# Hybrid encoder layer: first transfers in a held order, head norm weights spread on chip, first norms, value weights, bridge operands and closing sums reordered

## The chip, the cores and the metric

One core of a Trainium2 chip runs the kernel. It has a matrix engine (PE, TensorE) and three engines for the rest: DVE (VectorE), ACT (ScalarE) and POOL (GpSimd). SP (SyncE) issues most transfers, ACT some. Each engine works through its own instructions in order, and waits on semaphores for the others. The metric is the device time of one execution, in microseconds; lower is better.

## The reference

One layer of a pre-norm encoder, applied to two inputs with the same weights: `x_prompt` (1024 tokens) and `x_sample` (512 tokens), 1024 wide, float32.

```python
def _token_mixer(xn, w_in, q_norm_g, k_norm_g, rpb, w_proj_a, w_proj_b, w_out):
    z = xn @ w_in
    qa, ka, va, qb, kb, vb, ga, gb = jnp.split(z, idx, axis=-1)
    qa = _apply_rope(_rmsnorm(qa, q_norm_g), cos, sin)     # 8 heads of 64
    ka = _apply_rope(_rmsnorm(ka, k_norm_g), cos, sin)     # 2 heads
    o_a = _gqa_attention(qa, ka, va)                       # over all tokens
    o_b = _neighbourhood_attention(qb, kb, vb, rpb)        # 8 x 16 window, learned bias
    merged = jax.nn.sigmoid(ga) * (o_a @ w_proj_a) + jax.nn.sigmoid(gb) * (o_b @ w_proj_b)
    return merged @ w_out

def _trunk(x, ...):
    h = x + _token_mixer(_rmsnorm(x, norm_mix_g), ...)
    h = h + jnp.square(jax.nn.relu(_rmsnorm(h, norm_mlp_g) @ w_mlp_up)) @ w_mlp_down   # 4096 wide
    return _rmsnorm(h, norm_final_g)
```

## The kernel before

**Products.** Every product of float32 operands is three products on PE (`mm3`, lines 158 to 161). Each operand is split into a high half, rounded by a copy on ACT, and a low half, the difference, by a subtraction on DVE (`split`, lines 147 to 156; `cut`, 1074 to 1076, in the MLP). The three are high by high (L159), high by low and low by high (L160, L161).

**Trunks.** `run` handles a trunk: trunk 0 is `x_sample` (four tiles of 128 tokens; `first` is true), trunk 1 `x_prompt` (eight tiles). The profile's names read alike for both, so they are told apart by their times. Four stages follow each other in each:

- First (`phR`), in two groups of heads g = 0, 1: for each tile tt of 128 tokens the norm (`norm_tile`: squares summed on ACT, L214; `ms` on DVE, L142; the power on POOL, L144; the scaled tile `xn` on DVE, L218), eight transposes on PE into `ptx` (L232), and the split of these into `xs_0h` (ACT, L242) and `xs_0l` (DVE, L246). Then the product `z` with the weights of queries and keys, loaded by `load_a` (`rawq`, `rawkv`; halves `wgh`, `wgl`); the head norm (`sq` and `ssA` on ACT, L530; `ms_A`; `t` on DVE, L534, with the table `gtab`); the rotation with the rope tile `rt` (L552 to L554, result `rr`); and `heads_t`, transposes of `rr` into `pq` (L468). The key for the values is cut from `z` as `vhl` (L537, L538); that is the last reader of a tile's `z` and frees its PSUM buffer, of which there are four. `values` multiplies by the value weights that `load_v` loads (`raw_v`; halves `wh_v`, `wl_v`) into `zv`.
- Global attention (`phA`), with products of the gates as filling work for PE (`Fill`).
- Neighbourhood attention (`phB`): `load_qk(pr)` loads and splits the weights of a pair of heads (`raw_bq`, `raw_bk`; `w_bq`, `w_bk`), `qkproj` multiplies, and 32 units, four per head, run `s_unit` (scores `sb`, maximum, exponential `pb`, its sum's reciprocal `rlb` on DVE, L804, and `pb` scaled on POOL, L805), `t_unit` (transposes `ptb`, L817) and `v_unit`. Gate products `gps` with `w_gs` fill PE between.
- Projections, output weights and norms (`phG`).

**MLP.** `mlp` takes both trunks' 1536 tokens as two blocks of 768. `run_up(b, ...)` makes the up product of a block in 16 slices, as a scheme of seven smaller products (`ua` to `ud`) whose operands `A` and `B` are sums of blocks; what comes out (`c`, `cs`) goes to memory as `ud`. Between the blocks stands a **bridge** (lines 1384 to 1413): for q = 0, 1, 2 `pair_t` transposes a piece of the second block's `B` (`pt`, L270), and two of the down scheme's product 5, `dnf`, are made. Their operands come by `a_dma` (`ar`, from `ud`) and `a_step` (halves `ah`, `al`, L1075 and L1076). `last_of(0)` returns the steps that the last slice of the first block runs beside its products. After the second block come the down scheme's products in the order 5, 3, 1, 6, 7, 4, 2, with `gain` adding each result to the stream `h`, and `final`, `final_half` and `final_rest` making the closing norm.

**What sets the order.** The program is written for a tile scheduler, which builds each engine's list from the text's order, dependences and its own priorities; `tc.keep_in_program_order` holds an instruction at its place. A transfer waits at SP until its buffer is free, and until an earlier transfer, eight back, has landed, since each uses one of eight semaphores in turn.

**At the start** SP issues `xts_0` (tile 0), the norm weights, the query weights, `xts_1`, `rawkvs`, the head norm weights into `gtab` (the query's row of 64 read for 128 partitions and four heads), `raw_vs`, the first rope tile and only then `x23s` (tiles 2 and 3).

## Time and profile before

| what | us |
|---|---|
| median of three runs | 2198.17 (2197.47 to 2203.12) |
| the profiled execution | 2196.47 |
| its span, first to last instruction | 2194.7 |
| PE busy | 2137.7 |
| DVE busy | 1456.9 |
| ACT busy | 1111.3 |
| POOL busy | 348.0 |
| mean granted clock of PE | 0.994 |

How to read it: a row of a group or of the timeline names the line, the engine, the operation, `out<-in`, and in brackets the engine's idle time just before, with what ended it. The view of waits lists for PE which operation waited for which, the us in total, how often, and the longest. A row of the windows gives busy time of PE, its weight loads, DVE, ACT and POOL in a stretch, each with its count, then the granted clock of PE, the share of DMA time and GB/s. Times count from the start of the span. Line numbers are those of the kernel before.

### The profile page before, as it was taken

The page shows a single profiled execution, that of the slowest core. Times are in us where ns is not written, and L with a number is a line of the kernel's source. Part 1 is how long each engine was busy: PE and PEld are TensorE (multiplying, and loading weights), DVE is VectorE, ACT ScalarE, POOL GpSimd, SP SyncE. Part 2 cuts the span into 40 slices and gives each one's busy share as a digit, 9 for nine tenths or more (in the row PEclk, how much of TensorE's full clock was granted, in tenths as well). Part 3 has the DMA queues.
Part 4 walks back from the last instruction along what each step waited for, and adds up shares of the span by engine and source line. Part 5 has one row for each costly group of instructions (what it writes and reads, how often), then busy time and mean ns, then how long its engine had stood idle before and what let it go on. Part 6 is the DMA issues. An engine that isn't in the chain of part 4 may idle for free. (4 is left out here: it accounts for less than half of the span.)

```text
span 2194.7 us, 32408 instructions
## 1 busy us (share of the span) xinstructions
PE 2137.7 (97%) x11180; PEld 1869.9 (85%) x11180; DVE 1456.9 (66%) x2835; ACT 1111.3 (51%) x2377; POOL 348.0 (16%) x458
## 2 busy tenths in 40 slices
PE   6999999999999999999999999999999999999998
PEld 6787877898898888888888899997999988888886
DVE  5755567577756755545773777777777777769663
ACT  4645554456635655545531466665655543433452
POOL 2232120333333223223300200003000000000000
PEclk8999999999999999999999999999999999999999
DMA  5525548530122124324363556568544699788551
GB/s 150 165 84 156 150 138 270 196 91 30 44 68 90 42 60 126 97 84 125 122 200 136 199 181 192 175 226 205 172 142 157 214 351 341 235 275 282 178 193 67
DMA packets 320299, 351.56 MB, mean 160 GB/s; under 512 B 31751, under 2 KB 255623, under 8 KB 320135
## 3 DMA queue, kind: packets, MB, share of 16 engines
q1 hardware_dynamic: 278455, 280.27, 41.0%
q10 hardware_dynamic: 36000, 52.18, 6.8%
q0 software_dynamic: 5680, 17.04, 2.8%
q8 instruction: 88, 1.44, 0.3%
q14 instruction: 76, 0.62, 0.1%
HBM read 265.47 MB, written 87.88 MB: 161 GB/s over the span
## 5 line engine op out<-in xcount | busy, mean ns | idle before, releaser
L161 PE MATMUL dn<-wd,al 128*128 128x512 f32 x624 | 242.8, 389 | 0.0
L160 PE MATMUL dn<-wd,ah 128*128 128x512 f32 x624 | 242.8, 389 | 0.0
L159 PE MATMUL dn<-wd,ah 128*128 128x512 f32 x624 | 242.7, 389 | 0.0
L1075 ACT ACTIVATE ah<-ar 128x512 fp32r<-128x512 f32 x168 | 104.1, 628 | 197.6 <-PE dn L160 184.8
L1076 DVE TENSOR_TENSOR al<-ar,ah 128x512 fp32r<-128x512 f32 x168 | 115.4, 695 | 71.1 <-ACT ah L1075 61.7
L161 PEld LDWEIGHTS dn<-wd,al 128*128 128x128 f32 x624 | 117.1, 188 | 24.5
L159 PEld LDWEIGHTS dn<-wd,ah 128*128 128x128 f32 x624 | 117.1, 188 | 24.3
L160 PEld LDWEIGHTS dn<-wd,ah 128*128 128x128 f32 x624 | 117.1, 188 | 24.2
L634 DVE TENSOR_TENSOR ptls<-pTs,pths 128x512 fp32r<-128x512 f32 x160 | 107.5, 686 | 38.2 <-ACT pths L633 37.5
L594 POOL TENSOR_SCALAR ps<-ps,rls 128x1024 f32<-128x1024 f32 (+1 forms) x96 | 96.3, 1005 | 223.6 <-DVE rls L593 213.3
L633 ACT ACTIVATE pths<-pTs 128x512 fp32r<-128x512 f32 x160 | 94.2, 598 | 74.2 <-PE pTs L628 71.8
L588 DVE TENSOR_REDUCE nms<-ss 128x1 f32<-128x1024 f32 (+1 forms) x96 | 99.5, 1040 | 25.3 <-PE ss L586 25.3
L159 PE MATMUL gpss<-xs_0h,w_gs 128*128 128x512 f32 x256 | 106.1, 414 | 2.8 <-ACT sgs L363 1.3
L591 ACT ACTIVATE ps<-ss,nms 128x1024 f32<-128x1024 f32 (+1 forms) x96 | 93.3, 973 | 23.7 <-DVE nms L588 21.3
L628 PEld LDWEIGHTS pTs<-ident,ps 128*128 128x128 f32 x640 | 78.0, 140 | 29.0 <-POOL ps L594 4.5
L161 PE MATMUL gpss<-xs_0h,w_gs 128*128 128x512 f32 x256 | 101.6, 397 | 0.1
L160 PE MATMUL gpss<-xs_0l,w_gs 128*128 128x512 f32 x256 | 101.3, 396 | 0.0
L628 PE MATMUL pTs<-ident,ps 128*128 128x128 f32 x640 | 98.9, 274 | 1.3 <-DVE ptls L634 0.3
L144 POOL TENSOR_TENSOR rs_f<-ms_f,mhalf 128x1 f32<-128x1 f32 x6 | 4.0, 669 | 590.8 <-DVE ms_f L142 590.8
L805 POOL TENSOR_SCALAR pbs<-pbs,rlbs 128x384 f32<-128x384 f32 (+1 forms) x96 | 56.3, 592 | 226.0 <-DVE rlbs L804 211.7
L1076 DVE TENSOR_TENSOR A<-S,A 128x512 fp32r<-128x512 f32 x128 | 84.5, 686 | 9.6 <-ACT A L1075 9.4
L1075 ACT ACTIVATE A<-S 128x512 fp32r<-128x512 f32 x128 | 75.6, 623 | 29.5 <-DVE S L1138 21.6
(299 smaller groups left out, 6432.6 us busy)
## 6 DMA issues: line engine op xcount, KB each, us to landing
ar<-ud SPq DMA_DIRECT2D x120, 512.0 KB
br<-in_w_mlp_down_dram SPq DMA_DIRECT2D x72, 512.0 KB
rawu<-in_w_mlp_up_dram SPq DMA_DIRECT2D x64, 512.0 KB
ud<-c ACTq DMA_DIRECT2D x128, 192.0 KB
raw_gs<-in_w_in_dram SPq DMA_DIRECT2D x32, 512.0 KB
zgs<-sgs ACTq DMA_DIRECT2D x48, 256.0 KB
ud<-cs SPq DMA_DIRECT2D x64, 192.0 KB
raw_os<-in_w_out_dram SPq DMA_DIRECT2D x16, 512.0 KB
```

Of the source, the lines that this page charges most:

```text
L159: nc.tensor.matmul(out, ah, bh, start=start, stop=False, **kw)
L160: nc.tensor.matmul(out, ah, bl, start=False, stop=False, **kw)
L161: nc.tensor.matmul(out, al, bh, start=False, stop=stop, **kw)
L588: nc.vector.tensor_reduce(nm_, s, axis=AX.X, op=ALU.max, negate=True)
L591: nc.scalar.activation(p, s, AF.Exp, bias=nm_, accum_out=l)
L594: nc.gpsimd.tensor_scalar(p, p, rl, 1.0, op0=ALU.mult, op1=ALU.mult)
L628: nc.tensor.transpose(pt[:, j * P : (j + 1) * P], PP[u, j][:, kc * P : (kc + 1) * P], ident)
L633: nc.scalar.activation(hi, pt, AF.Copy)
L634: nc.vector.tensor_tensor(lo, pt, hi.bitcast(F32), op=ALU.subtract)
L805: nc.gpsimd.tensor_scalar(p, p, rl, 1.0, op0=ALU.mult, op1=ALU.mult)
L1075: nc.scalar.activation(hi, src, AF.Copy)
L1076: nc.vector.tensor_tensor(lo, src, hi.bitcast(F32), op=ALU.subtract)
```

## The change

It has five parts.

- **Start, trunk 0.** `x23s` is held in place and issued behind `rawkvs`; the norm of tile 1 is written ahead of the split of `rawkvs`. The query's head norm weights are loaded once as `gq` (64 per partition), and the multiplication that fills `gtab` reads them broadcast over four heads. Several first transfers are held in program order.
- **Value weights, trunk 1.** Their splits are collected in `hold` and run after tile 0's rotation; the norm of tile 4, the first that is made there, comes after tile 1's rotation.
- **Neighbourhood attention.** `load_qk(1)` moves from ahead of unit 0 to unit 3.
- **Bridge.** The last slice of the first block makes four operands of product 5 instead of two; each step of the bridge issues the next step's loads ahead of `pair_t` and splits its operands a step ahead.
- **Closing sums.** `final_rest` is cut in two, and its scaling runs after the next `gain`.

```diff
     def setup_tables():
-        row_bcast(gtab[:, 0:4, :], w["a_q_norm_g"], HD, 4)
-        row_bcast(gtab[:, 4:5, :], w["a_k_norm_g"], HD, 1)
+        gq = sgp.tile([P, 512], F32, tag="sg", name="gq", bufs=2)[:, 0:HD].rearrange("p (o d) -> p o d", o=1)
+        tc.keep_in_program_order(row_bcast(gq, w["a_q_norm_g"], HD))
+        tc.keep_in_program_order(row_bcast(gtab[:, 4:5, :], w["a_k_norm_g"], HD))
         tc.keep_in_program_order(
-            nc.vector.tensor_scalar(gtab[:, 0:4, :], gtab[:, 0:4, :], 0.125, None, op0=ALU.mult)
+            nc.vector.tensor_scalar(gtab[:, 0:4, :], gq.to_broadcast([P, 4, HD]), 0.125, None, op0=ALU.mult)
         )
...
-            split(hi[:, kk : kk + kn, :], lo[:, kk : kk + kn, :], rv)
+            cut = partial(split, hi[:, kk : kk + kn, :], lo[:, kk : kk + kn, :], rv)
+            if hold is None:
+                cut()
+            else:
+                hold.append(cut)
...
-                    xn_of[tr.ready] = norm_tile(xt, gb, ph, f"{N}_{tr.ready}")
+                    if first:
+                        xn_of[0] = norm_tile(xt, gb, ph, f"{N}_0")
...
+                    def more_and_norm():
+                        more_x()
+                        xn_of[1] = tr.p0(1, ph, gb, x1.pop())
+
-                    wh, wl = load_a(g, lambda: x1.append(norm_load(x, 1, ph, f"{N}_1")), first_tile, more_x)
+                    wh, wl = load_a(g, lambda: x1.append(norm_load(x, 1, ph, f"{N}_1")), first_tile, more_and_norm)
...
-                if first and fresh:
-                    xn_of[1] = tr.p0(1, ph, gb, x1.pop())
...
                     rr_of[tt] = rr
+                    while held:
+                        held.pop(0)()
+                    if fresh and not first and tt == 1:
+                        xn_of[tr.ready] = norm_tile(xt, gb, ph, f"{N}_{tr.ready}")
...
-            wqk = load_qk(1)
...
+                if i == 3:
+                    wqk = load_qk(1)
...
-                        more = [lambda: a_step(5, 0, 0), lambda: a_step(5, 0, 1)]
+                        more = [lambda g_=g_, j=j: a_step(5, g_, j) for g_ in range(2) for j in range(2)]
...
         for q in range(3):
+            if q < 2:
+                for g in range(2):
+                    a_dma(5, g, q + 1)
             pair_t(f"1_{q}", q, hn.pop(q), B, [bank(f"pt1_{q}_{i}") for i in range(4)], t2)
...
-                    n = 4 * q + 2 * g + i + 2
-                    if n < 12:
-                        a_step(5, n // 2 % 2, n // 4 * 2 + n % 2)
+                    if q < 2:
+                        a_step(5, g, j + 2)
...
-                    final_rest(NTB + j)
+                    final_rest(NTB + j, scales)
+        while scales:
+            scales.pop(0)()
```

What the scheduler makes of it is seen in the engines' lists. First SP at the start of the program, before (the names are those of the text above; `in_...` are inputs):

```order
L207 DMA xts_1_159<-in_x_sample_dram 128x1024
L404 DMA rawkvs_0_197<-in_w_in_dram 128x8x64 x2
L108 DMA gtab<-in_a_q_norm_g_dram 128x4x64
L108 DMA gtab<-in_a_k_norm_g_dram 128x64
L183 DMA raw_vs_0_0_220<-in_w_in_dram 128x4x256
L183 DMA raw_vs_0_4_227<-in_w_in_dram 128x4x256
L506 DMA rts_0_0_257<-in_rope_dram 128x128
L444 DMA x23s_200<-in_x_sample_dram 128x1024 x2
L506 DMA rts_0_1_355<-in_rope_dram 128x128
```

And now:

```order
L216 DMA xts_1_159<-in_x_sample_dram 128x1024
L413 DMA rawkvs_0_197<-in_w_in_dram 128x8x64 x2
L455 DMA x23s_200<-in_x_sample_dram 128x1024 x2
L109 DMA gq<-in_a_q_norm_g_dram 128x64
L109 DMA gtab<-in_a_k_norm_g_dram 128x64
L186 DMA raw_vs_0_0_221<-in_w_in_dram 128x4x256
L186 DMA raw_vs_0_4_228<-in_w_in_dram 128x4x256
L522 DMA rts_0_0_258<-in_rope_dram 128x128
L522 DMA rts_0_1_356<-in_rope_dram 128x128
```

`x23s` has moved ahead of both head norm weights, the value weights and the first rope tile, and the query's row is 128x64 instead of 128x4x64. ACT at the same place, before (`L148` and `L150` are the split's copy, `L214` and `L223` a norm's squares, `L242` and `L251` the split of a transposed tile, `L530` and `L548` the sums of the head norm):

```order
L148 ACTIVATE wghs_0_0_151<-rawkvs_0_197 128x4x128
L148 ACTIVATE wghs_0_1_155<-rawkvs_0_197 128x4x128
L214 ACTIVATE xns_1_209,sss_1_210<-xts_1_159 128x1024
L148 ACTIVATE wh_vs_0_0_222<-raw_vs_0_0_220 128x1024
L148 ACTIVATE wh_vs_0_0_222<-raw_vs_0_4_227 128x1024
L214 ACTIVATE xns_2_249,sss_2_250<-x23s_200 128x1024
L242 ACTIVATE xs_0h_167<-ptxs_1_236 128x4x128
L242 ACTIVATE xs_0h_168<-ptxs_1_236 128x4x128
L530 ACTIVATE sqs_0_0_308,ssAs_0_0_309<-zs_0_0_259 128x64 x5
L242 ACTIVATE xs_0h_167<-ptxs_2_334 128x4x128
```

And now:

```order
L223 ACTIVATE xns_1_203,sss_1_204<-xts_1_159 128x1024
L150 ACTIVATE wghs_0_0_151<-rawkvs_0_197 128x4x128
L150 ACTIVATE wghs_0_1_155<-rawkvs_0_197 128x4x128
L251 ACTIVATE xs_0h_167<-ptxs_1_237 128x4x128
L251 ACTIVATE xs_0h_168<-ptxs_1_237 128x4x128
L223 ACTIVATE xns_2_250,sss_2_251<-x23s_200 128x1024
L150 ACTIVATE wh_vs_0_0_223<-raw_vs_0_0_221 128x1024
L150 ACTIVATE wh_vs_0_0_223<-raw_vs_0_4_228 128x1024
L548 ACTIVATE sqs_0_0_309,ssAs_0_0_310<-zs_0_0_260 128x64 x5
L251 ACTIVATE xs_0h_167<-ptxs_2_335 128x4x128
```

Tile 1's norm stands ahead of the splits of `rawkvs`, its split ahead of tile 2's norm, and the value weights (`wh_vs`) behind both. On DVE the multiplication of `gtab` and tile 2's `xn` likewise stand behind tile 1's split and ahead of the value weights' low halves. The second place is DVE at the start of trunk 1, before:

```order
L154 TENSOR_TENSOR wl_vs_0_0_4791<-raw_vs_0_0_4788,wh_vs_0_0_4790 128x512 x2
L154 TENSOR_TENSOR wl_vs_0_0_4791<-raw_vs_0_4_4795,wh_vs_0_0_4790 128x512 x2
L142 TENSOR_SCALAR ms_s_4_4760<-sss_4_4758 128x1
L218 SCALAR_TENSOR_TENSOR xns_4_4757<-xts_4_4754,rs_s_4_4762,gbs_4753 128x1024
L142 TENSOR_SCALAR ms_As_0_0_4838<-ssAs_0_0_4832 128x5
L534 SCALAR_TENSOR_TENSOR ts_0_0_4842<-zs_0_0_4806,rs_As_0_0_4840,gtab 128x64 x5
L142 TENSOR_SCALAR ms_As_0_1_4891<-ssAs_0_1_4885 128x5
L495 TENSOR_TENSOR vts_0_0_4962<-zvs_0_0_4937,vts_0_0_4962 128x4x64
L538 TENSOR_TENSOR vhls_0_4803<-zs_0_0_4806,vhls_0_4803 128x64
L552 TENSOR_TENSOR ts_0_0_4842<-ts_0_0_4842,rts_0_0_4804 128x320
```

And now:

```order
L144 TENSOR_SCALAR ms_As_0_0_4825<-ssAs_0_0_4819 128x5
L552 SCALAR_TENSOR_TENSOR ts_0_0_4829<-zs_0_0_4793,rs_As_0_0_4827,gtab 128x64 x5
L156 TENSOR_TENSOR wl_vs_0_0_4784<-raw_vs_0_0_4781,wh_vs_0_0_4783 128x512
L556 TENSOR_TENSOR vhls_0_4790<-zs_0_0_4793,vhls_0_4790 128x64
L156 TENSOR_TENSOR wl_vs_0_0_4784<-raw_vs_0_0_4781,wh_vs_0_0_4783 128x512
L156 TENSOR_TENSOR wl_vs_0_0_4784<-raw_vs_0_4_4785,wh_vs_0_0_4783 128x512
L570 TENSOR_TENSOR ts_0_0_4829<-ts_0_0_4829,rts_0_0_4791 128x320
L156 TENSOR_TENSOR wl_vs_0_0_4784<-raw_vs_0_4_4785,wh_vs_0_0_4783 128x512
L572 TENSOR_TENSOR rrs_0_0_4841<-ts_0_0_4829,us_0_0_4837 128x320
```

The low halves `wl_vs` have moved from ahead of tile 0's head norm to places between it and its rotation, tile 4's norm (`xns_4`) to behind these rows; on ACT tile 0's sums likewise now stand ahead of the copies `wh_vs`. The third place is DVE in the neighbourhood attention of trunk 0, before:

```order
L797 ISA sbss_0_1_0_2286,nmbs_0_1_0_2287<-sbs_0_1_2281,bms_0_1_0_2282 128x256
L797 ISA nmbs_0_1_0_2287 128x1
L762 TENSOR_TENSOR kBs_0_1_2200<-pkbs_0_0_2236,kBs_0_1_2200 64x512 x2
L154 TENSOR_TENSOR w_bqs_1_2271<-raw_bqs_1_0_2269,w_bqs_1_2271 128x512 x2
L154 TENSOR_TENSOR w_bks_1_2277<-raw_bks_1_0_2275,w_bks_1_2277 128x512 x2
L804 RECIPROCAL rlbs_0_1_0_2292<-lbs_0_1_0_2290 128x1
L154 TENSOR_TENSOR w_gs_3328_1_2316<-raw_gs_3328_1_0_2314,w_gs_3328_1_2316 128x512 x2
```

And now:

```order
L819 ISA sbss_0_1_0_2275,nmbs_0_1_0_2276<-sbs_0_1_2270,bms_0_1_0_2271 128x256
L819 ISA nmbs_0_1_0_2276 128x1
L784 TENSOR_TENSOR kBs_0_1_2201<-pkbs_0_0_2237,kBs_0_1_2201 64x512 x2
L826 RECIPROCAL rlbs_0_1_0_2281<-lbs_0_1_0_2279 128x1
L819 ISA sbss_0_2_0_2328,nmbs_0_2_0_2329<-sbs_0_2_2325,bms_0_1_0_2271 128x256
L819 ISA nmbs_0_2_0_2329 128x1
L156 TENSOR_TENSOR w_gs_3328_1_2305<-raw_gs_3328_1_0_2303,w_gs_3328_1_2305 128x512 x2
L826 RECIPROCAL rlbs_0_2_0_2334<-lbs_0_2_0_2332 128x1
```

The splits of the next pair's weights no longer stand ahead of the first reciprocal; those of two gates' weights and of `w_bqs_1` follow behind it. In the bridge the low halves `al` of the second and the later steps now stand ahead of the products that use them by a whole step. On DVE, ACT, POOL and SP the list of the closing sums (`gain`, the sums, the scaling) is the same before and after.

## The prediction, made before the changed kernel was run

> **What bounds the kernel now.** The page's first part says whose time it is:

> ```profile
> PE 2137.7 (97%) x11180; PEld 1869.9 (85%) x11180; DVE 1456.9 (66%) x2835; ACT 1111.3 (51%) x2377; POOL 348.0 (16%) x458
> ```

> PE is busy for 97% of the span, so an edit pays only where PE stands idle or runs slowly. The number of matrix products does not change. I therefore went to the waits of PE (columns: total us, times, longest us):

> ```profile
> PE ptxs L232 <- DVE xns L218: 13.8, 4, 10.5
> PE zs L159 <- DVE vts L495: 3.9, 1, 3.9
> PE dnf L161 <- DVE al L1076: 2.9, 3, 1.5
> PE ptbs L817 <- POOL pbs L805: 2.4, 2, 1.4
> ...
> PE gpss L159 <- ACT w_gs L148: 0.7, 1, 0.7
> ```

> The first four rows are the sites of the diff: first norms, value weights, bridge, neighbourhood attention; the last belongs to the fourth. Then I read the timeline around each, and the windows for the granted clock (PEclk, third column from the right). A drop of it is a second price of a gap.

> **Start: first norms and transfers.** The queue of SP, then ACT, DVE and PE (start, duration; in brackets the idle time before and its releaser):

> ```profile
> 3.43 3.76 SPq L404 DMA_DIRECT2D rawkvs<-in_w_in_dram  x2
> 7.23 3.54 SPq L108 DMA_DIRECT2D gtab<-in_a_q_norm_g_dram  x1
> ...
> 17.04 1.49 SPq L444 DMA_DIRECT2D x23s<-in_x_sample_dram  x2
> ```
> ```profile
> 10.65 1.07 ACT L242 ACTIVATE xs_0h<-ptxs 128x512 fp32r<-128x512 f32 x2
> 13.12 1.15 ACT L148 ACTIVATE wghs<-rawkvs 128x512 fp32r<-128x512 f32 x2 [1.41 <-DMA rawkvs<-in_w_in_dram]
> 14.18 1.05 ACT L214 ACTIVATE xns<-xts 128x1024 f32<-128x1024 f32 x1
> ...
> 22.03 1.06 ACT L148 ACTIVATE wh_vs<-raw_vs 128x1024 fp32r<-128x1024 f32 x1 [6.71 <-DMA raw_vs<-in_w_in_dram]
> ...
> 25.85 1.06 ACT L214 ACTIVATE xns<-x23s 128x1024 f32<-128x1024 f32 x1 [1.29 <-DMA x23s<-in_x_sample_dram]
> ```
> ```profile
> 20.43 0.29 DVE L114 TENSOR_SCALAR gtab<-gtab 128x256 f32<-128x256 f32 x1 [2.98 <-DMA gtab<-in_a_q_norm_g_dram]
> ...
> 28.01 1.29 DVE L246 TENSOR_TENSOR xs_0l<-ptxs,xs_0h 128x512 fp32r<-128x512 f32 x2 [2.12 <-ACT xs_0h L242]
> ...
> 30.02 1.28 DVE L218 SCALAR_TENSOR_TENSOR xns<-x23s,rs_s,gbs 128x1024 f32<-128x1024 f32 x1 [0.66 <-POOL rs_s L144]
> ```
> ```profile
> 31.36 1.97 PE L232 MATMUL ptxs<-ident,xns 128*128 128x128 f32 x8 [10.51 <-DVE xns L218]
> ```
> ```profile
> 20.85:31.36 10.51, 0.01 (x2) 0.01 (x1) 5.28 (x9) 5.26 (x16) 0.55 (x1) 0.56 0.88 260
> 31.36:36.00 4.64, 4.64 (x18) 4.64 (x19) 2.13 (x9) 2.24 (x5) 2.34 (x3) 0.54 0.00 0
> ```

> PE has multiplied tile 0 and stands for 10.51 us until tile 2's norm is there, because `x23s` was issued only at 17.04. The next 4.64 us ran at 0.54 of the clock: 4.64 x 0.46 = 2.1 us more. After the change `x23s` follows `rawkvs`, at about 7.2. Its 1.05 MB at the window's 260 GB/s take 4.0 us; behind weights used at 13.12 they are there at 15 to 17. What is late next is ACT and DVE, in the new order:
> - Tile 1's Square follows `xs_0h` at 11.7 instead of 14.18, so its norm (1.05, then sum and power, 0.8 from 29.21 to 30.02 for tile 2, then 1.28) ends near 15. Its own split now stands ahead of tile 2's norm: transposes about 1.0, `xs_0h` 1.07, to 17.5; then Square 1.06 with `xs_0l` beside it, 0.8, and `xns` 1.28 behind the 0.29 of L114. Tile 2 is ready at about 21.2, and PE starts it 31.36 - 21.2 = **10.2** earlier, with a wait of 1 to 2 us in place of 10.51.
> - A wait of that size cost no clock at the bridge and some at the neighbourhood attention (both below): I take the **2.1** back whole, and 0 as the lower end.
> - `wh_vs` (two times 1.06) stand on ACT ahead of the heads' sums and of tile 2's split. If `raw_vs` lands near 22 as now, tile 2's low half is about **1.5** late for PE, and tile 3's norm, queued behind the same work, about **1**.

> 10.2 + 2.1 - 1.5 - 1 = **9.8 us**. Bounds: 12.3 without the last two; 4 if tile 2 lands 4 us later (the whole 1 MB once more) and no clock comes back. Broadcasting on DVE costs nothing I can price: L114 keeps its 128x256 output at 0.29 us, and `xns` is the only work behind it that PE awaits.

> **Value weights, trunk 1.** ACT, DVE, PE, and the window behind:

> ```profile
> 422.44 2.01 ACT L148 ACTIVATE wh_vs<-raw_vs 128x1024 fp32r<-128x1024 f32 x2
> 425.52 1.06 ACT L214 ACTIVATE xns<-xts 128x1024 f32<-128x1024 f32 x1 [1.07 <-DMA xts<-in_x_prompt_dram]
> ```
> ```profile
> 423.79 2.49 DVE L154 TENSOR_TENSOR wl_vs<-raw_vs,wh_vs 128x512 fp32r<-128x512 f32 x4
> ...
> 431.68 0.21 DVE L538 TENSOR_TENSOR vhls<-zs,vhls 128x64 fp32r<-128x64 f32 x1
> ```
> ```profile
> 431.81 0.69 PE L159 MATMUL zs<-wghs,xs_0h 128*128 128x384 f32 x1 [3.85 <-DVE vts L495]
> ```
> ```profile
> 431.81:436.00 4.19, 4.19 (x20) 3.78 (x20) 2.16 (x10) 1.44 (x4) 2.91 (x5) 0.62 0.42 137
> ```

> Tile 3's product needs the accumulator of tile 0, freed by `vhls` at 431.68, because tile 0's head sums wait on ACT behind `wh_vs` and tile 4's Square, which waited for its DMA. At stake: 3.85 + 4.19 x 0.38 = 5.4 us. Now the sums come first, 4 us earlier, and free it near 427.5. But the low halves of the value weights now stand on DVE behind tile 0's scaling and, the last, behind its rope multiplication: four times 0.62 with those between ends near 429 instead of 426.3, and PE's value product, due at 424.9, is queued ahead of tile 3. PE then waits in several short pieces and reaches tile 3 about 1 us earlier; some of the clock comes back. I take **1.5** (0 to 4). In the second group three whole products lie ahead of the values (20 matmuls of one fill 4.19 x 0.62 = 2.6 us at full clock, so 9 us for 72) and hide the held splits: 0.

> **Neighbourhood attention.** DVE, ACT, PE, the window and SP, trunk 0:

> ```profile
> 202.74 1.29 DVE L154 TENSOR_TENSOR w_bqs<-raw_bqs,w_bqs 128x512 fp32r<-128x512 f32 x2
> 203.95 1.28 DVE L154 TENSOR_TENSOR w_bks<-raw_bks,w_bks 128x512 fp32r<-128x512 f32 x2
> 205.16 0.15 DVE L804 RECIPROCAL rlbs<-lbs 128x1 f32<-128x1 f32 x1
> ...
> 215.42 0.16 DVE L804 RECIPROCAL rlbs<-lbs 128x1 f32<-128x1 f32 x1 [0.54 <-ACT pbs L802]
> ```
> ```profile
> 201.19 1.04 ACT L148 ACTIVATE w_bqs<-raw_bqs 128x1024 fp32r<-128x1024 f32 x1
> 202.14 1.05 ACT L148 ACTIVATE w_bks<-raw_bks 128x1024 fp32r<-128x1024 f32 x1
> ...
> 203.58 1.04 ACT L148 ACTIVATE w_gs<-raw_gs 128x1024 fp32r<-128x1024 f32 x1
> ```
> ```profile
> 206.82 0.69 PE L817 MATMUL ptbs<-ident,pbs 128*128 128x128 f32 x2 [1.41 <-POOL pbs L805]
> ```
> ```profile
> 206.80:210.00 3.20, 3.18 (x9) 2.64 (x10) 1.26 (x7) 1.36 (x5) 2.24 (x4) 0.54 0.14 40
> ```
> ```profile
> 190.88 17.67 SPq L707 DMA_DIRECT2D vss<-vds  x16
> ```

> The reciprocal stands behind two splits of 1.29 and 1.28 for the next pair; without them it comes 2.4 us earlier and the 1.41 goes. The same splits on ACT, 1.04 and 1.05, stood ahead of `w_gs` (0.7). Clock: 3.20 x 0.46 = 1.5. Together 3.6; later reciprocals now have gate splits and `w_bqs` ahead of them, for which I take off 0.6: **3.0** (1 to 4). Trunk 1 has the other `ptbs` wait (2.4 - 1.4 = 1.0): **0.7** (0 to 1). Of the moved loads `raw_bks` now stands on SP behind the 16 `vss`, whose row ends at 208.55, so it is issued there. Its product comes after unit 7: unit 0 has its reciprocal at 205.16, unit 4 at 215.42, so unit 7 near 223, and 14 us lie between. The split is hidden; without that cover PE would wait for it one for one.

> [...]

> **Bridge.** DVE and PE at one of the three waits:

> ```profile
> 1494.31 1.27 DVE L282 TENSOR_TENSOR B<-pt,B 128x512 fp32r<-128x512 f32 x2
> 1495.51 0.67 DVE L1076 TENSOR_TENSOR al<-ar,ah 128x512 fp32r<-128x512 f32 x1
> ```
> ```profile
> 1496.23 0.50 PE L161 MATMUL dnf<-wd,al 128*128 128x512 f32 x1 [0.83 <-DVE al L1076]
> ```

> `al` is made behind the `B` splits and just too late, three times, 2.9 us in all; no clock is lost there. In the new order two pairs are split before `c` of the last slice, and each later pair stands a whole step ahead of its 24 products. The added splits (four of 0.67) replace the same ones later; they could hold up the end of the first block by part of that. I take **2.5** (0.5 to 3.2: a little of the work behind may come earlier too).

> **Closing sums: 0.** `gain`, `edge_t`, `yl` stand on DVE in the same alternation before and after, so the scheduler already did what the text now says.

> **Sum.** 9.8 + 1.5 + 3.0 + 0.7 + 2.5 = 17.5. The profiled execution took 2196.47 (span 2194.7): 2179.0. The median of the runs shown, 2198.17, is 1.7 higher: 2180.7. I forecast **2180**. PE is the bound behind each site, so what is won there stays won.

> **The rivals.**
> - *A new wait takes the place at the start* (16%). On DVE the L114 multiplication now stands ahead of tile 2's norm. If the broadcast still lands at 20.43, `xns` ends near 23 and PE waits 3.5 us, near the 3.85 behind which trunk 1 lost its clock, so the clock drops too: 1.8 + 2.1 less, 2184; if the heads' sums also come late behind `raw_vs`, 2188. For it: ACT waited 6.71 for `raw_vs` that followed this broadcast. Against: only a quarter of that transfer is left.
> - *The change does not do what it says elsewhere* (6%). As at the closing sums, nothing is won at the bridge and trunk 1, and start and neighbourhood give half: 4.9 + 1.8, so 2190 to 2191.5.
> - *The clock behind the 1.41 gap does not come back* (25%, counted inside the forecast's 74%). The rows alone allow it: `dnf`'s 1.53 lost no clock. 2181.5.
> - *Slower: `raw_vs` last in the held order* (4%). ACT is in order, and `wh_vs` stands ahead of tile 2's `xs_0h`, needed for every later tile. Now `x23s` and both broadcasts come before it. Past about 24 each us of lateness is one us of PE. It eats all 17.5 if `raw_vs` lands past 41.5; at 44, 2200. Nothing in the rows shows a transfer that long at the start, and its issue comes earlier than 11.5 if anything.

> **How the numbers follow.** The forecast has 74%, and its own bounds add up to 2172 (12.3 + 4 + 4 + 1 + 3.2) and 2192.7 (4 + 0 + 1 + 0 + 0.5, from the median), hardly all at once. I take 2173 to 2191, which also holds most of the first rival. A difference below 0.3%, 6.6 us, cannot be told from none: the line is 2191.6. Faster 0.88: forecast, the first rival and part of the second, less a little. Same 0.08, slower 0.04.

> **What would show it.** Right: the `ptxs` wait falls from 13.8 to about 4, its longest to 2, and PE starts tile 2 at 21 to 22; the clock stays full in the 30s; `ptbs` and `dnf` leave the list or fall below 0.5; a `zvs` wait on `wl_vs` replaces the 3.9 one; the tail behind PE's last product stays 8.5 us. Wrong: PE idle for 3 us or more at tile 2, a wait for `wh_vs` or `gtab`, a clock drop behind the value product as large as before, or new waits of `ud` at the end of the first block.

## The result, and the profile after

| what | before | after |
|---|---|---|
| median, us | 2201.1 (6 runs, 2197.47 to 2203.52) | 2182.8 (6 runs, 2179.18 to 2184.21) |
| profiled execution, us | 2196.47 | 2184.21 |
| span of it, us | 2194.7 | 2182.4 |
| mean granted clock of PE in it | 0.994 | 0.994 |

The medians differ by 18.3 us; the ratio is 0.9916, with an interval of 0.9903 to 0.993, which is 15 to 21 us. Only fast executions count in this and all later ratios: one of the eleven of the kernel with the bridge alone and `dp` in another pool (below) took 7435 us and is left out. Note the profiled executions: that of before is the fastest of all its runs, that of after the slowest. They differ by 12.3 us, and a comparison of the two traces can only account for these. Where the rest lies is a question of its own, taken up under "The four parts, each alone".

PE does the same products, and its waits have changed. The page of the kernel after, first part, and its waits of PE (total us, times, longest us):

```profile
PE 2140.7 (98%) x11180; PEld 1874.7 (86%) x11180; DVE 1456.6 (67%) x2835; ACT 1110.5 (51%) x2377; POOL 351.8 (16%) x458
```
```profile
PE ptxs L241 <- DVE xns L227: 3.8, 4, 1.6
PE ub L161 <- ACT A L1098: 3.7, 2, 3.0
PE ss L607 <- ACT kTs L490: 2.6, 4, 2.0
...
PE ops L161 <- ACT mgs L973: 2.0, 1, 2.0
PE zvs L162 <- DVE wl_vs L156: 1.8, 1, 1.8
...
PE ptbs L839 <- POOL pbs L827: 0.7, 1, 0.7
```

`ptxs` has gone from 13.8 to 3.8, its longest from 10.5 to 1.6; `ptbs` from 2.4 to 0.7; the `zs` wait of 3.9 on `vts` has become a `zvs` wait of 1.8 on `wl_vs`; `dnf` has left the list. But `ub` has a wait of 3.0 that before did not have (before: 1.0 in all).

The same start as in the prediction, now SP, ACT, DVE and PE of the kernel after (start, duration, idle before and its releaser):

```profile
7.17 4.02 SPq L455 DMA_DIRECT2D x23s<-in_x_sample_dram  x2
...
12.26 0.93 SPq L186 DMA_DIRECT2D raw_vs<-in_w_in_dram  x2
```
```profile
17.43 1.09 ACT L251 ACTIVATE xs_0h<-ptxs 128x512 fp32r<-128x512 f32 x2 [3.12 <-PE ptxs L241]
18.40 1.06 ACT L223 ACTIVATE xns<-x23s 128x1024 f32<-128x1024 f32 x1
...
21.15 1.06 ACT L150 ACTIVATE wh_vs<-raw_vs 128x1024 fp32r<-128x1024 f32 x1 [0.65 <-DMA raw_vs<-in_w_in_dram]
```
```profile
19.76 0.28 DVE L116 TENSOR_SCALAR gtab<-gq 128x256 f32<-128x256 f32 x1
...
20.77 1.28 DVE L227 SCALAR_TENSOR_TENSOR xns<-x23s,rs_s,gbs 128x1024 f32<-128x1024 f32 x1 [0.67 <-POOL rs_s L146]
```
```profile
22.11 1.37 PE L241 MATMUL ptxs<-ident,xns 128*128 128x128 f32 x8 [1.61 <-DVE xns L227]
```

Tile 2's transposes start at 22.11 instead of 31.36. Neither `x23s` nor the broadcast `gq` is waited for any more: ACT takes `x23s` without idle time, DVE takes `gtab` without idle time. What PE waits for is the chain of Square, `ms`, power and `xns` itself.

The lead of the kernel after over that of before, from the two profiled executions: the start of each product in before, less the start of the same product in after.

| at (us of before) | lead | what came since the row above |
|---|---|---|
| 110 | 9.7 | start |
| 196 | 9.3 | +2.5 and -2.9: see `ss` below |
| 224 | 14.2 | neighbourhood attention, trunk 0 |
| 370 | 9.1 | three waits, at `gpss`, `ppas` and `ops`, and half clock behind the last, 357.29 to 360.70 |
| 460 | 11.5 | value weights, trunk 1 |
| 840 | 11.5 | |
| 1290 | 12.4 | `pt` |
| 1525 | 17.8 | bridge, while its products run |
| end | 12.2 | first products behind the bridge |

### The profile page after: what moved, and what is told of

It reads as the page before. It is cut to its first block, busy times and chain, and to the rows that moved or that the text cites. A ratio compares the mean times of both kernels' runs of the same rounds, so it can differ in the third digit from the quotient of the medians.

```text
span 2182.4 us, 32426 instructions
## 1 busy us (share of the span) xinstructions
PE 2140.7 (98%) x11180; PEld 1874.7 (86%) x11180; DVE 1456.6 (67%) x2835; ACT 1110.5 (51%) x2377; POOL 351.8 (16%) x458
## 3 DMA queue, kind: packets, MB, share of 16 engines
q0 software_dynamic: 5680, 17.04, 2.8%
## 5 line engine op out<-in xcount | busy, mean ns | idle before, releaser
L161 PE MATMUL dn<-wd,ah 128*128 128x512 f32 x624 | 242.7, 389 | 0.0
L161 PEld LDWEIGHTS dn<-wd,ah 128*128 128x128 f32 x624 | 117.1, 188 | 24.4
L161 PE MATMUL gpss<-xs_0h,w_gs 128*128 128x512 f32 x256 | 105.9, 414 | 2.2 <-ACT sgs L372 1.3
```

Of the source, the lines that this page charges most:

```text
L161: nc.tensor.matmul(out, ah, bh, start=start, stop=False, **kw)
```

## The four parts, each alone

Each kernel is the kernel before with one part of the change. The closing part has none: on DVE, ACT, POOL and SP its lists are those of before, so nothing in their order has changed, and it was not run. The other four shared 26 runs of before, median 2202.7 us (2199.83 to 2205.33).

**Start alone.** The head norm weights, the held order of the transfers and tile 1's norm.

```diff
+            tc.keep_in_program_order(nc.sync.dma_start(x23[:, i, :], ...))
...
+        xn_of[1] = tr.p0(1, ph, gb, x1.pop())   # in more_and_norm
...
+        tc.keep_in_program_order(row_bcast(gq, w["a_q_norm_g"], HD))
```

> The kernel before with the start's part of the change alone (held transfers, head norm weights spread on chip, tile 1's norm ahead). Theory A (the parts add, each worth the lead that PE gains at its place): the changed kernel's trace shows PE 9.7 us ahead of before at 110 us, so 9.7 us faster, 8 to 11.5 with the clock's chance. Theory B (the lead at the start is partly given back where later stages wait for their own transfers): 5 us or less. The longest ptxs wait is 1.6 under both.

Measured: 2189.93 us, ratio 0.994 (0.9929 to 0.9952), 12.8 us faster: more than theory A's 8 to 11.5, and theory B falls. In its profile the lead is 9.1 at 60 us and 9.6 at 110, as forecast, and no product waits for a low half of `raw_vs` there.

**Neighbourhood attention alone.**

```diff
-            wqk = load_qk(1)
...
+                if i == 3:
+                    wqk = load_qk(1)
```

> The kernel before with the neighbourhood attention's part alone (loads and splits of the next pair at unit 3). Theory A: the lead grows from 9.3 to 14.2 between 196 and 224 us and loses 1.2 by 260, and 0.3 comes in trunk 1: 4.0 us faster (3 to 5). Theory B (my prediction's 3.7 was right by its own terms, ptbs waits and clock): the ptbs waits of 2.4 fall below 1 and the clock stays full from 206 to 210. Theory C (the lead there comes from an earlier clock phase of the changed kernel and not from the edit): under 2 us, with the clock dropping at 206 as before.

Measured: 2195.9 us, ratio 0.9973 (0.9963 to 0.9983), 6.8 us faster, above the 3 to 5 of theory A. The window that ran at 0.54 before, in the kernel with this part alone:

```profile
206.80:210.00 3.20, 3.20 (x20) 2.72 (x19) 2.33 (x8) 1.38 (x5) 1.99 (x4) 1.00 1.03 289
```

The 1.41 us gap is gone and PE runs at full clock: theory C falls, and with this edit alone the clock here is 1.00 where it was 0.54.

**Value weights alone.** The splits held, and tile 4's norm later.

```diff
+                held = None if first else []
...
+                    while held:
+                        held.pop(0)()
+                    if fresh and not first and tt == 1:
+                        xn_of[tr.ready] = norm_tile(xt, gb, ph, f"{N}_{tr.ready}")
```

> The kernel before with the value weights' part alone (splits held back, tile 4's norm later, in trunk 1). Theory A: in the changed kernel the lead grows by 2.4 us between 420 and 460 although the clock still drops there once (behind a wait of 1.8 for the low halves): 2.4 us faster, a wait zvs on wl_vs of 1.5 to 2. Theory B: whether the clock falls behind that wait is chance; where it does not, 4 us faster. Theory C: held splits only move the wait: under 1 us.

Measured: 2198.7 us, ratio 0.9983 (0.9975 to 0.9992), 4.0 us faster. PE waits 2.5 us for `wl_vs` in two pieces in place of one of 3.9, and in this profile the clock stays full behind them (1.00 from 426 to 438), as in theory B.

```profile
PE zvs L161 <- DVE wl_vs L155: 2.5, 2, 1.8
```

**Bridge alone.**

```diff
-                        more = [lambda: a_step(5, 0, 0), lambda: a_step(5, 0, 1)]
+                        more = [lambda g_=g_, j=j: a_step(5, g_, j) for g_ in range(2) for j in range(2)]
...
+            if q < 2:
+                for g in range(2):
+                    a_dma(5, g, q + 1)
             pair_t(...)
...
+                    if q < 2:
+                        a_step(5, g, j + 2)
```

> The kernel before with the bridge's part alone. Theory A (from the changed kernel's trace: PE gains 5.4 us in the bridge and gives back 5.5, because the sums ta of the next step wait in a buffer that the previous step's dp still holds until its transfer hd has landed, 4.1 and 6.2 us on DVE, and the operands of the second block come late: ub waits 3.0): no change within 1 us, a ub wait of about 3. Theory B (my prediction): 2.5 us faster, and the 3.0 at ub is chance of that one run.

Measured: 2202.72 us, ratio 0.9997 (0.9988 to 1.0006): nothing. The wait for `al` is gone, and in the waits of PE of this kernel stands a new one:

```profile
PE ub L160 <- ACT A L1090: 4.3, 2, 3.6
```

**What the parts add up to.** 12.8 + 6.8 + 4.0 + 0 = 23.6 us, while the whole gave 18.3, and in a second measurement (below) 20.4. Each part is known to within some 2 to 2.5 us either way, so the two agree roughly; I don't explain their difference.

**Why medians show more than the two profiles.** The kernel with the bridge alone has the start and the trunks of before. Yet in its profile (2205.32 us) its products are 5.9 us behind those of the profiled execution of before at 460, and 7.8 at 1440, ahead of the bridge. One place of this is the projection of trunk 0. PE in before, then in the bridge alone, and there the window behind:

```profile
367.36 0.50 PE L159 MATMUL ops<-wh_os,mgs 128*128 128x512 f32 x1 [0.80 <-ACT mgs L950]
```
```profile
370.95 0.50 PE L160 MATMUL ops<-wh_os,mgs 128*128 128x512 f32 x1 [1.76 <-ACT mgs L965]
371.60:375.01 3.41, 3.41 (x9) 2.66 (x9) 1.85 (x5) 2.67 (x3) 0.00 (x0) 0.50 0.89 302
```

The same wait is 0.80 in one execution and 1.76 in the other; the second also costs half the clock for 3.41 us. The profiled execution of before had the good side of several such places. This is also what the row "370" of the lead's table shows: kernel after had 2.0 us at `ops` in its profiled execution, and 0.7 in the next one measured:

```profile
PE ops L161 <- ACT mgs L973: 0.7, 1, 0.7
```

Matched against the same profile of before, that execution keeps a lead of 14.3 to 15.3 from 222 to 420 and has 16.6 at 460, where the profiled one fell from 14.2 to 9.1 and had 11.5. So this loss belongs to the execution, not to the change.

## The bridge: where 5 us went

After the bridge the second block waits. DVE of the kernel after, then PE:

```profile
1494.22 0.69 DVE L304 TENSOR_TENSOR ta<-pt,ta 128x512 f32<-128x512 f32 x1 [4.09 <-DMA hd<-dp]
...
1510.59 0.69 DVE L304 TENSOR_TENSOR ta<-pt,ta 128x512 f32<-128x512 f32 x1 [6.18 <-DMA hd<-dp]
```
```profile
1516.45 0.45 PE L161 MATMUL ub<-B,A 128*128 128x384 f32 x1 [3.02 <-ACT A L1098]
```

DVE needs a buffer for `ta`, a sum inside `pair_t`, and waits for a transfer that adds `dp`, a result of product 5, to the stream. `dp`, `ta`, `ah`, `al`, `y` and `S` share one pool, `k2`, of 14 buffers, taken in turn. The view of the tile `dp`, of before and of after (who waited for it, in us and times, and its transfers' time to landing):

```profile
DVE S L1140: 0.2, 1
...
DMA to landing us min/median/max: 5.2/6.1/8.3
```
```profile
DVE ta L304: 10.3, 2
...
DMA to landing us min/median/max: 4.0/8.7/11.2
```

In the new order more operands stand between a `dp` and the next `ta`; the turn comes round to a `dp` buffer whose transfer is still running. The transfer holds the buffer, `ta` holds `B`, and then `S`, `A` and `ub`. The theory: the reordering wins 5 us and the shared pool takes them back. The rival: the bridge had nothing to win. The test gives `dp` buffers of another pool (`rw`, through `raw4`; the expectations call it `raw`, the pool of the raw up weights), once in the kernel after and once in the kernel with the bridge alone. The first ran beside the kernel after, unchanged, and two more below; these shared 9 runs of before, 2202.53 us.

```diff
-                t = t2(f"dp{j}")
+                t = raw4(f"dp{j}")[:, 0:512]
```

> The changed kernel once more, on one chip with three kernels that differ from it in one place each. The four parts alone gave 12.8, 6.8, 4.0 and 0 us by their medians, 23.6 in sum. Theory A (the parts add): 20 us or more faster than before on this chip. Theory B (some of it is the same clock drops counted twice, since start and neighbourhood attention each rid the program of the drops behind their gap, and drops elsewhere come instead): 17 to 19, as in the first comparison, with 5 or more half-rate stretches left in the trace.

Measured: 2182.14 us (2178.65 to 2183.24), ratio 0.9905 (0.9891 to 0.9918), 20.4 us faster, with two windows of half clock ahead of the program's end (mean granted clock 0.998, against 0.994 in the first profile of this kernel): by little on the side of theory A.

> The changed kernel with one edit: the bridge's results dp take a buffer from the pool of the raw up weights instead of the one that the sums ta of the next step share. Theory A (the wait of ta for dp's transfer is what gives the bridge's gain back): DVE's waits of 4.1 and 6.2 us at ta go, ub's wait falls from 3.0 to below 1, and the kernel is 4 us faster than the changed one (3.0 and a clock drop of 1.7 behind it; 2.5 to 5.5). Theory B (ub waits because the raw up weights arrive late in the bridge, whatever ta does): ub still waits 2 or more, no gain, or slower, since the raw pool now holds dp too.

Measured: 2176.41 us (2173.36 to 2178.32), ratio 0.9878 (0.9864 to 0.9892), 5.7 faster than the kernel after beside it. In the profile the lead over the kernel after grows from 2.5 to 7.7 at the end of the bridge, at no other place by as much; the two `ta` have no idle time before them, and of the `ub` wait this is left:

```profile
PE ub L161 <- ACT A L1098: 0.7, 1, 0.7
```

> The kernel before with the bridge's reordering alone, and the products' results dp in buffers of the pool raw instead of k2. Theory A (the reordering wins about 5 us at the low halves al, which shared buffers give back): 4 to 6 us faster than before, 2196.5 to 2198.5, no ub wait over 1 us at the bridge. Theory B (the 5 us that the changed kernel gained with these buffers came from elsewhere): at most 1.5 us faster than before.

This kernel, the next one and two more below shared 15 runs of before, 2201.47 us. Measured: 2195.87 us, ratio 0.9974 (0.9965 to 0.9983), 5.6 faster than before, against nothing for the same reordering in shared buffers. The theory holds from both sides. From the last product of the first block to the first `ub` it takes 44.9 us in the profile of before, 39.8 here, and the same products gain 5.1 us (from 7.7 behind before to 2.6); 3.2 of the 5.1 are idle time of PE in pieces of 0.3 us and more. The other 1.9 I did not follow; four of the 48 transposes of this stretch (`pt`) now stand ahead of its start.

> The changed kernel with dp in buffers of raw, once more, beside the other three: 2174 to 2179 again, ratio to the kernel before 0.986 to 0.9895; the ub wait at the bridge below 1 us again.

Measured: 2175.95 us (2175.14 to 2176.75), ratio 0.9884 (0.9871 to 0.9898). This is the best version: 5.7 us better than the kernel after where the two ran side by side, 4.6 by the ratios of this second measurement (0.9884 against 0.9905).

## The start and the value weights, taken apart

**The broadcast over four heads put back** into the kernel after:

```diff
-        tc.keep_in_program_order(row_bcast(gq, w["a_q_norm_g"], HD))
+        tc.keep_in_program_order(row_bcast(gtab[:, 0:4, :], w["a_q_norm_g"], HD, 4))
```

> The changed kernel with the query's head norm weights read from memory for four heads again (128x4x64), in the same held place behind x23s. Theory A (the first rival of my prediction: the slow broadcast then ends ahead of tile 2's norm on DVE, 8 us after the tiles that now precede it, near 24): tile 2's norm starts near 25 instead of 20.8, PE waits 5 to 6 instead of 1.6, 4 to 6 us slower than the changed kernel. Theory B (the order of the transfers alone does it, the size of the broadcast does not matter): less than 1 us.

Measured: 2188.52 us (2186.72 to 2188.86), ratio 0.9933 (0.992 to 0.9945), 6.4 slower than the kernel after beside it. DVE and PE:

```profile
25.20 0.29 DVE L115 TENSOR_SCALAR gtab<-gtab 128x256 f32<-128x256 f32 x1 [5.13 <-DMA gtab<-in_a_q_norm_g_dram]
```
```profile
26.74 1.97 PE L240 MATMUL ptxs<-ident,xns 128*128 128x128 f32 x8 [6.08 <-DVE xns L226]
```

128 KB in pieces of 256 bytes come 5 us too late, and as the multiplication stands on DVE ahead of tile 2's norm, PE stands for 6.08. That is the wait of my first rival. But the size of the broadcast is not all that differs. SP of this kernel:

```profile
7.29 3.59 SPq L131 DMA_DIRECT2D pad<-in_b_rel_pos_bias_dram  x1
13.31 0.75 SPq L136 DMA_DIRECT2D shifted<-pad  x2
14.11 0.86 SPq L454 DMA_DIRECT2D x23s<-in_x_sample_dram  x2
15.01 0.43 SPq L109 DMA_DIRECT2D gtab<-in_a_q_norm_g_dram  x1
```

Transfers of the bias now stand ahead of `x23s`, and the broadcast is issued at 15.01, where `gq` was issued at 11.23. `x23s` still came in time (ACT takes it at 18.56, against 18.40). From its issue to DVE's use the broadcast took 10.2 us here, and 13.2 in before (7.23 to 20.43). Issued at 11.23 it would be there at 21.4 to 24.4, an estimate from these two, so 1.3 to 4.4 us late instead of 5.13. The broadcast over four heads is thus too slow for this place by itself, but the 6.4 us are the price of its size and its later issue together; no run here parts them.

**Tile 1's norm put back** behind the split of `rawkvs`, in the kernel after:

```diff
-                        xn_of[1] = tr.p0(1, ph, gb, x1.pop())
...
+                if first and fresh:
+                    xn_of[1] = tr.p0(1, ph, gb, x1.pop())
```

> The changed kernel with tile 1's norm written behind the split of rawkvs again. Theory A: tile 1's norm comes 1.3 to 2 us later on DVE and PE waits for it near 16 as before (1.6); tile 2 then starts later by about the same: 1 to 2 us slower than the changed kernel. Theory B (tile 2 is held by ACT and DVE, not by tile 1's place): under 0.5 us, with the wait only moved from 20.5 to 16.

Measured: 2184.74 us (2183.58 to 2185.66), ratio 0.9917 (0.9903 to 0.993). At its place the wait only moves: 1.64 us ahead of tile 1 instead of 1.61 ahead of tile 2, and the lead there is 0.2 us smaller. The other part of the 2.6 us lies at places that change between executions (2.9 us at `ops` in this profile), so this run settles no more than that the norm's place is worth little where it stands: by its time it lies outside both theories, by its trace it is theory B.

**The value weights' splits not held**, in the kernel after and in the best version:

```diff
-                held = None if first else []
+                held = None
```

> The changed kernel, but the splits of the second trunk's value weights are not held (they run where they are written); only the norm of tile 4 stays behind tile 1's rotation. Theory A (the tile's norm was what kept the accumulator; the held splits only added the value product's waits of 1.8 and 0.7 us): the zvs waits on wl_vs go, the zs wait comes back with at most about 1 us, and the kernel is 1 to 2 us faster than the changed one, 2180 to 2181.5. Theory B (holding the splits is what frees the accumulator): a zs wait of 2.5 to 4 us comes back at trunk 1's start, with a half-rate stretch behind it in the profiled run; 1 to 3 us slower than the changed kernel, 2183 to 2186.

Measured: 2180.72 us (2180.44 to 2184.45), ratio 0.9912 (0.9899 to 0.9926). Against the kernel after (0.9905) the times tell nothing, though the number is the one that theory A named. But the wait did come back, as in theory B, now with tile 4's norm out of the way:

```profile
416.05 0.41 PE L161 MATMUL zs<-wghs,xs_0h 128*128 128x384 f32 x1 [2.84 <-DVE vhls L556]
```

> The changed kernel with both edits: dp in buffers of raw, and the value weights' splits not held. If the two act apart, and the first theory of the unheld splits holds, it is 1 to 2 us faster than the changed kernel with dp in raw alone, 2174.5 to 2175.5; if the second holds, 1 to 3 us slower than that, 2177.5 to 2179.5.

Measured: 2178.12 us (2175.75 to 2180.32), ratio 0.9894 (0.9881 to 0.9908), 2.2 slower than the best version beside it (2175.95), with ranges that overlap a little and intervals that overlap for the most part, so the times point to theory B without showing it. Its profile shows the 2.8 us `zs` wait too. From 418 to 470 us the two profiles without held splits gain 0.3 and 0.1 us on before, the second execution of the kernel after 1.9 and the best version 1.4. By these traces the splits have to be held to free the accumulator in time; moving the norm alone brings the wait from 3.85 down to 2.84 only.

## Why the prediction was right, and where it was wrong

The forecast of 2180 and the measured 2182.8 lie close in part by luck. The median that it started from, 2198.17 of three runs, was 2.9 below the 2201.1 of six. The gain of 17.5 that it took off is near the measured 18.3 because its errors met: the bridge's 2.5 came to nothing, and the three other parts, measured alone, were each worth more than their terms, 12.8 against 9.8, 6.8 against 3.7 and 4.0 against 1.5, of which some was lost again when the parts came together (23.6 against 18.3). Between the two profiled executions the gain was 12.3.

- **Start, 9.8: right in size.** The lead was 9.7, by 9.25 for tile 2 (22.11, where the text had 21.2), and nothing lost at `raw_vs` and tile 3's norm, for which it took off 2.5: `wh_vs` waited only 0.65 us for its transfer. The 2.1 of the clock, taken back whole, didn't come back in the profiled execution, though it did in the next (see the last section). Three small misses cancelled. Alone it measured 12.8 in medians, 10.6 to 15.6 by its interval.
- **Value weights, 1.5: right in kind, low in size.** The wait for `wl_vs` that the text named came, 1.8 us. 2.4 us were won between the profiles (9.1 to 11.5), 4.0 (1.8 to 5.5) in medians by the part alone. What the medians add I can only point at: in the profile of the bridge alone (mean granted clock 0.989) the gap at this place of before is 4.05 us long, with two windows of half clock behind it (436.4 to 443.3), in that of before (0.994) 3.85, with one (431.62 to 435.03). In the profiled execution of the kernel after the clock falls for one window behind the value product, as it did in the kernel before. That is one of the signs that the text had listed as wrong; in the second execution of the same kernel it stays full there (1.00 from 418.70 to 422.10).

```profile
418.73:422.14 3.41, 3.41 (x17) 3.35 (x16) 2.93 (x8) 1.71 (x12) 1.78 (x3) 0.50 0.54 155
```

- **Neighbourhood attention, 3.0 and 0.7: right in kind, the first low.** The lead rose by 4.9 at its place, from 9.3 to 14.2. The sum left out two waits of before, of 0.52 and 0.53 us (below this item), that are gone as well. Of the 0.6 taken off for gates' splits ahead of later reciprocals 0.3 came, as a wait of `ptbs` for `rlbs`. The third rival (the clock stays lost) fell, by the window at 1.00. `ptbs` on `pbs` fell to 0.7, not below 0.5. Trunk 1's 0.7 did not show: nothing between 460 and 840. The part alone measured 6.8 (3.7 to 8.1).

```profile
216.03 0.51 PE L794 MATMUL sbs<-kBs,qBs 128*128 128x256 f32 x2 [0.52 <-DVE nmbs L797]
217.07 0.50 PE L159 MATMUL gpss<-xs_0h,w_gs 128*128 128x512 f32 x1 [0.53 <-DMA vss<-vds]
```

- **Bridge, 2.5: wrong.** The step that failed is "I take 2.5 (0.5 to 3.2)". It priced the `al` that come earlier and asked whether the added splits hold up DVE; it did not ask in which buffers the earlier operands stand. With four operands in flight the pool of 14 came round to buffers that POOL's transfers still held. It won 5.4 in the profile (12.4 to 17.8) and gave back 5.5, the 3.0 us wait and a window of half clock behind it (1517.82 to 1521.23) among these. Of the signs that the text listed as wrong none was this one. And the size of what the reordering itself wins was low: with `dp` in other buffers it was worth 5.6 alone, where the text allowed 3.2 at most.
- **Closing sums, 0: right.** The lists are the same.
- **From profile to median, "1.7 higher".** The step used three runs. Over 26 and 9 and 15 further runs the median of before is 2202.7, 2202.53 and 2201.47, 5 to 6 above the profiled execution. From the 2201.1 measured beside the kernel after, the same sum would have given 2183.6.
- **The rivals.** The first did not happen: the row read once came in time, and with the row read for four heads, and issued later, its wait came. The second (nothing at bridge and trunk 1) was half true, for the bridge; the one on the clock fell at the place that it spoke of; `raw_vs` was not late.

A cost that the text did not name: at 134.9 PE waits 1.97 us for `kTs` (`ss`), and the clock is half for 3.4 us behind it (135.42 to 138.83). ACT, which makes `kTs`, stands behind the values' pieces `vts`, late on DVE behind splits of a gate's weights that the scheduler put there. Before had 2.32 at `pqs` instead, ending at 126.1, with full clock (1.00 from 126.1 to 131.2). The kernel with the start alone has the same wait; those with one of the other three parts alone don't, so it comes with the start:

```profile
PE ss L604 <- ACT kTs L489: 2.6, 4, 2.0
```

No kernel was made against it, so the rest of the cause is read from the trace alone.

## What to carry to other kernels

Where operands are made earlier, count the buffers that they take in turn and ask whose transfer still holds the next one: an edit that removed 2.9 us of waits and opened the way to 5 gave all of it back through a shared pool, and one changed line brought it back. A profile is one execution; where waits of 1 to 3 us decide, compare medians for the size and several profiles for the place. A small broadcast in short pieces took 10 to 13 us from issue to use here: it belongs behind everything that the matrix engine needs first, or on chip.

## What the runs showed of the hardware

| profile | half clock, us | idle time of PE in the window ahead, us |
|---|---|---|
| before | 22.02 to 35.67 | 1.17 |
| before | 206.34 to 209.75 | 1.67 |
| before | 431.62 to 435.03 | 3.41 |
| after | 12.54 to 15.96 | 1.73 |
| after | 22.78 to 26.20 | 1.61 |
| after | 135.42 to 138.83 | 1.97 |
| after | 357.29 to 360.70 | 2.01 |
| after | 418.73 to 422.14 | 1.80 |
| after | 1517.82 to 1521.23 | 2.05 |

Of the windows that full clock followed, the one with the most idle time had 1.70 us in before (124.42 to 127.83) and 1.45 in after (1248.17 to 1251.58). Two executions of the kernel after differ behind the same wait. First the window with the 1.61 us gap and the one behind it, in the profiled execution:

```profile
19.37:22.78 3.41, 1.80 (x17) 1.66 (x16) 2.74 (x6) 2.77 (x11) 0.55 (x1) 1.00 0.85 209
```
```profile
22.78:26.20 3.42, 3.42 (x14) 3.42 (x13) 2.13 (x6) 2.56 (x9) 1.18 (x1) 0.50 0.43 122
```

And in the second one:

```profile
19.34:22.75 3.41, 1.80 (x15) 1.66 (x15) 2.80 (x4) 2.94 (x13) 0.55 (x1) 1.00 0.90 225
```
```profile
22.75:26.16 3.41, 3.41 (x21) 3.41 (x21) 2.12 (x9) 1.87 (x5) 1.20 (x2) 1.00 0.64 176
```

1.80 us busy in both, then half clock in one and full in the other: 14 records of products against 21 in the same time. A window of half clock costs 3.41 x 0.5 = 1.7 us, an estimate from these rows, and the same wait of the same kernel was followed by it in one execution and not in the other.

The counts also fit what the prediction left open, why 1.41 us cost the clock at the neighbourhood attention and 1.53 at the bridge did not. The windows of before at both places:

```profile
202.90:206.34 3.44, 1.76 (x8) 1.00 (x6) 3.44 (x7) 2.33 (x5) 0.93 (x1) 1.00 0.06 23
```
```profile
1506.81:1510.22 3.41, 2.34 (x18) 1.96 (x17) 3.41 (x5) 3.41 (x8) 1.27 (x1) 1.00 0.57 108
1510.22:1513.63 3.41, 2.95 (x13) 2.44 (x14) 2.80 (x5) 0.88 (x3) 0.00 (x0) 1.00 0.51 155
```

The first holds the 0.74 us wait for `w_gs` and most of the 1.41: 1.68 us idle of 3.44, and of the windows with 1.5 to 1.76 half clock followed 11 and full clock 21. At the bridge the end of a window cuts the 1.53 us gap in two, 1.07 and 0.46, both far below those.
